# Last up-projection unit to first down products: where three operand casts and two weight casts stand in the queues

## Chip, cores and metric

One Trainium2 chip, one core. The metric is device time in microseconds (us), median over runs. The engines' names are those of the profile: PE (matrix multiplication), PEld (its weight loads), DVE (vector), ACT (scalar), POOL (GpSimd), SP (the queue that issues most DMA transfers). Each engine works through its own instructions strictly in the order in which the compiled program lists them, and an instruction that waits holds all behind it.

## What is computed

One layer for 1024 prompt frames and 32 sample frames (T = 1056 columns here): attention and a gated recurrence side by side, then a convolutional feed-forward block, then a gated per-layer input. The change lies in the feed-forward block:

```python
hf = _rms_norm(x, g_pre_ffn)
a, u = jnp.split(hf @ w_up, 2, axis=-1)          # 1024 -> 2 * 2816
ap = jnp.concatenate([prev, a], axis=1)
ac = b_conv
for j in range(CONV_W):                          # depthwise conv3
    ac = ac + ap[:, j:j + t] * w_conv[j]
ffn = (jax.nn.gelu(ac, approximate=True) * u) @ w_down   # 2816 -> 1024
x = x + _rms_norm(ffn, g_post_ffn)
```

All is float32. PE multiplies in a rounded format, so each operand is split in a rounded part (a cast on ACT) and the rest (a subtraction on DVE), and each product is three matmuls: rounded times rounded, rounded times rest, rest times rounded.

## The kernel before

**Up units.** The up-projection runs in 22 units u = 0..21 (NF = 22), each 128 columns of `a` and of `u`. A unit multiplies by a seven-product scheme (sums of quarter blocks stand in for the eighth product): `up_unit` goes through seven steps, each with a weight part `wt` of 4 x 128 x 128, two halves p of the tokens (264 columns each, on 128 partitions), in three PSUM tiles X, Y, Z. One step is 24 matmuls of 128x264. Behind its steps a unit leaves a tail, `ff_tail`: on DVE the scaling of u (L2264), the last sum out of PSUM (L2401) and its scaling into `ab` (L2405, L2408), copies of a few columns (L2254 to L2257); then the convolution, one tap on ACT (L2258) and two on DVE (L2262, L2266), the gelu on ACT (L2267), the product with u on DVE (L2271), a store. For all but the last unit this tail runs beside the next unit's matmuls.

**Down products.** The down-projection takes the same scheme over three groups of rows of `w_down`. The first group (pt = 0) has 3 blocks of 128 in each part. It runs in two phases: the products i = 0, 1, 2 for the column groups c = 0..3, then i = 3..6. So the down parts in order are: part 0, 1, 2 for c = 0; 3, 4, 5 for c = 1; 6, 7, 8 for c = 2; 9, 10, 11 for c = 3. One part is 18 matmuls. `d_unit` runs the products of one c: product 0 goes to PSUM tile X, product 1 to Y, and product 2 is added onto X. In between, `evacuate` copies X as it stands after product 0 to `S` on ACT (L2514), so that **product 2 of a c can't start before the `S` copy of that c has read X**. Y goes to `T`, and X after product 2 to `acc`, both also L2514 on ACT.

**Operands.** Product i needs two operand tiles `dop` (p = 0, 1), loaded by POOL's queue (`load_op`), cast on ACT (L2344) and completed on DVE (L2345) by `split_ops`. A weight part needs a raw tile `wd` (one tile holds two parts, two buffers, loaded by SP's queue, L2124), a cast on ACT (L2135) into a `wt` tile, and the rest on DVE (L2136): `d_prepare`. The `wt` tiles rotate over eight buffers, so that a cast may also have to wait for PE to finish with an old part. A third raw tile can be loaded only when both parts of the tile two before it have been cast and completed.

**What sets the order.** Instructions stand in a queue in the order in which the scheduler of the compiler puts them, from the order in which they are written; `behind(E)` keeps what is written under it behind the last instruction written so far for that engine. In the last unit (u = 21) the loads and casts of the first down products stand between the steps.

The functions around the change:

Of the kernel before, what the change touches and what calls it, by code (L numbers as in the profile page):

```python
# [59 lines left out]
def layer_kernel(  # L60
# [17 lines left out]
    def nm(s):  # L78
        n_names[0] += 1
        return f"{s}_{n_names[0]}"  # L80
# [5 lines left out]
    V, S, G, E = nc.vector, nc.scalar, nc.gpsimd, nc.tensor  # L86

    def behind(*engines):

        st = ExitStack()  # L90
        for e in engines:
            ins = next(i for i in reversed(nc.cur_bb.bb.instructions) if i.engine == e.engine)
            st.enter_context(tc.issue_after(ins))
        return st
# [1955 lines left out]
    def part_tile(i=0):  # L2050
        return wp.tile([P, 2, 4, P], F32R, tag="wb", name=nm("wt"), bufs=8)
# [62 lines left out]
    def d_raw():  # L2114

        k = len(raw_d)
        t = wp.tile([P, KT, P], F32, tag="wr", name=nm("wd"), bufs=2)
        raw_d.append(t)
        for a in range(2):
            pt, c, i = D_ORDER[2 * k + a]  # L2120
            j0, n = KP[pt]
            z_ = slice(j0, j0 + n)
            src = w_d[i][:, c, z_] if i in w_d else dv[:, i // 2 % 2 + i // 5, i // 5, c, z_]
            dma(t[:, 4 * a:4 * a + n], src)  # L2124

    def d_prepare(n):

        while len(ready_d) < min(n + 1, len(D_ORDER)):
            k = len(ready_d)
            while len(raw_d) < min(k // 2 + 2, len(D_ORDER) // 2):  # L2130
                d_raw()
            ng = KP[D_ORDER[k][0]][1]
            src = raw_d[k // 2][:, 4 * (k % 2):4 * (k % 2) + ng]
            t = part_tile()
            S.copy(t[:, 0, :ng], src)  # L2135
            V.tensor_tensor(t[:, 1, :ng], src, t[:, 0, :ng].bitcast(F32), op=ALU.subtract)  # L2136
            ready_d.append(t)
# [140 lines left out]
    def tail_rest(u):  # L2278
        for t in tail_of:
            next(t)  # L2280
        if u != 1:
            tail_of.clear()
# [58 lines left out]
    def split_op(pt, p, i):  # L2341
        n = KP[pt][1]
        hi, lo = (ops[p][i][:, a, :n] for a in range(2))
        S.copy(hi, lo.bitcast(F32))  # L2344
        V.tensor_tensor(lo, lo.bitcast(F32), hi.bitcast(F32), op=ALU.subtract)  # L2345

    def split_ops(pt, i, ps=(0, 1)):
        for p in ps:
            with behind(S, V):
                split_op(pt, p, i)  # L2350
# [3 lines left out]
    def up_unit(u):  # L2354
        X, Y, Z = (pf.tile([P, 2, 512], F32, tag="st", name=nm("st"), bufs=3) for _ in range(3))
        ab = fp.tile([P, 4 + T], F32, tag="ab", name=nm("ab"), bufs=2)
        G.memset(ab[:, 0:2], 0.0)
        us = us0 if u == 0 else Up[:, u % 2, :].bitcast(F32)
        us4 = us.rearrange("p (a h c) -> p a h c", a=2, h=2)
        w = {}  # L2360

        def mults(i, t, first, ps):
            n = 7 * u + i
            if i not in w:
                w[i] = ready_w[n]
            for p in ps:
                for k in range(4):
                    wh, wl = w[i][:, 0, k, :], w[i][:, 1, k, :]
                    xh, xl = ops[p][i][:, 0, k, :], ops[p][i][:, 1, k, :]
                    o = t[:, p, 0:H]  # L2370
                    E.matmul(o, wh, xh, start=first and k == 0, stop=False, skip_group_check=True)  # L2371
                    E.matmul(o, wh, xl, start=False, stop=False, skip_group_check=True)  # L2372
                    E.matmul(o, wl, xh, start=False, stop=k == 3, skip_group_check=True)  # L2373

        def v(t, ps):
            return t[:, ps[0]:ps[-1] + 1, 0:H]

        def after(i, ps):
            x, y, zz = v(X, ps), v(Y, ps), v(Z, ps)
            sl = slice(ps[0], ps[-1] + 1)  # L2380
            s1 = s10[:].unsqueeze(1) if u == 0 and ps == (0,) else s1c[:, sl]
            if i == 0:
                S.copy(s1, x)  # L2383
            elif i == 1:
                V.tensor_tensor(U2[:, sl], s1, y, op=ALU.subtract)
            elif i == 2:
                V.tensor_tensor(ab[:, 2:2 + T].rearrange("p (a h c) -> p a h c", a=2, h=2)[:, sl, 0, :],
                                x, rb4[:, sl, 0, :], op=ALU.mult)
            elif i == 3:
                V.tensor_tensor(nU3[:, sl], y, s1, op=ALU.subtract)  # L2390
            elif i == 4:
                V.tensor_tensor(us4[:, sl, 1, :], nU3[:, sl], zz, op=ALU.subtract)
            elif i == 5:
                V.tensor_tensor(us4[:, sl, 0, :], y, s1, op=ALU.subtract)
            elif i == 7:

                S.copy(t12[:, sl], zz)
            elif i == 8:
                V.tensor_tensor(nU3[:, sl], nU3[:, sl], t12[:, sl], op=ALU.add)
            else:  # L2400
                V.tensor_tensor(t12[:, sl], U2[:, sl], zz, op=ALU.add)  # L2401

        def done():

            V.tensor_tensor(ab[:, 2:2 + T].rearrange("p (a h c) -> p a h c", a=2, h=2)[:, :, 1, 0:232],  # L2405
                            t12[:, :, 0:232], rb4[:, :, 1, 0:232], op=ALU.mult)
            for p, o in ((0, 2 + 496), (1, 2 + 1026)):
                V.tensor_tensor(ab[:, o:o + 32], t12[:, p, 232:H], rb4[:, p, 1, 232:H], op=ALU.mult)  # L2408
            tail_of.append(ff_tail(u, ab, us))
            next(tail_of[0])  # L2410


        order = ((0, X, True, (0,)), (1, Y, True, (1,)), (2, X, False, (2,)), (3, Y, False, (3,)),
                 (4, Z, True, (4,)), (5, Y, False, (5,)), (6, Z, False, (6,)))
        first_ = order[:2] + ((2, X, False, ()),) + order[3:6] + ((6, Z, False, (2, 6)),)
        early = ((0, X, True, (0,)), (6, Z, True, (7,)), (2, X, False, ()), (1, Y, True, (1,)),
                 (3, Y, False, (3, 8)), (4, Z, False, (4, 6)), (5, Y, False, (2, 5)))
        for ps, steps in (((0,), first_), ((1,), early)) if u == 0 else (((0, 1), order),):
            for n, (i, t, first, then) in enumerate(steps):
                if u == NF - 1 and n == 0:  # L2420
                    d_raw()
                    d_raw()
                if u:
                    prepare(min(7 * u + n + AHEAD, 7 * NF - 1))
                    if u == NF - 1 and n:
                        d_prepare(n - 1)
                elif ps == (1,):
                    with behind(S, V):
                        prepare(n + AHEAD + 2)
                mults(i, t, first, ps)  # L2430
                if u == NF - 1:
                    if i < 3:
                        for p in range(2):
                            load_op(0, p, i, gdma)
                    if n in (3, 5, 6):
                        split_ops(0, {3: 0, 5: 1, 6: 2}[n])
                if ps == (1,) and n == 1:
                    with behind(E):
                        x1_t.append(pair_norm(1, 1.0 / D, late=True))
                if ps == (1,) and n == 4:  # L2440
                    with behind(E):
                        x1_t[0]()
                for a in then:
                    with behind(*((V,) if ps == (0,) and a == 2 else ())):
                        after(a, ps)
                if n == 1:
                    with behind(V):
                        tail_rest(u)
                if u == 1 and n == 3:
                    with behind(V):  # L2450
                        tail_rest(0)
                if u > 1 and n == 2 + u % 2:
                    if u % 2 == 0:
                        sums_of.append(act_sums(u // 2 - 1))
                    with behind(V):
                        next(sums_of[-1])
                if u == 0 and ps == (0,):
                    last_ops(n)
                if 2 <= u < 18 and n in (1, 4):
                    w_sum((u - 2) // 2, 2 * (u % 2) + n // 4)  # L2460
        done()

    Up = None
    for u in range(NF):
        if u == 1:
            Up = page(lq, 2, [P, 2, T], "Up")
        up_unit(u)
    tail_rest(NF)
    fctx.close()
    foctx.close()  # L2470
# [476 lines left out]
```

## Time and profile before

| what | value |
|---|---|
| time, median of 3 runs | 1944.42 us (1942.07, 1944.42, 1945.03) |
| the profiled execution's own time | 1947.46 us |
| its span, that is first to last instruction | 1945.8 us |
| mean granted PE clock | 0.996 |
| PE busy, of the span | 99% |
| DVE, ACT, POOL busy, of the span | 76%, 53%, 20% |
| last matmul of the last up unit starts at | 1602.00 us |
| matmuls of the down products | from 1602.1 to 1832.8 us |

The profiled execution is 3.04 us longer than the median of the runs, 1.66 us of it outside the span. Times of rows below count from the span's start. A row of the timeline gives start, duration, engine, line, output and inputs, shapes, and in brackets how long the engine had been idle before it and what released it. PE's rows overlap: a matmul of 128x264 lasts 0.28 us, and one starts about every 0.12 us.

### The profile page before, as it was taken

To read this page: it belongs to the slowest core of one execution; us is meant where nothing else is said; L and a number is where in the kernel's file an instruction comes from. 1 tells how busy PE (TensorE), PEld (TensorE's weight loads), DVE (VectorE), ACT (ScalarE), POOL (GpSimd) and SP (SyncE) were. 2 spreads that over 40 slices of the span, in tenths; PEclk is the share of its full clock that TensorE was granted. 3 is DMA by queue.
4 is the path that set the end of the run, shared out by engine and by line. 5 is a ranking of instruction groups with operands and counts; after the bars stand their busy time and mean duration, and the time that the engine had idled before them with its cause. 6 is when DMAs were issued, how large, how long until landed. Compare 5 with 4: busy or idle time off the path is not lost.

```text
span 1945.8 us, 38169 instructions
## 1 busy us (share of the span) xinstructions
PE 1921.6 (99%) x14523; PEld 1903.9 (98%) x14523; DVE 1472.6 (76%) x3201; ACT 1028.7 (53%) x2214; POOL 381.4 (20%) x530
## 2 busy tenths in 40 slices
PE   8999999999999999999999999999999999999999
PEld 7999999999999999999999999999999999999998
DVE  5777777788888888755796878777787786768872
ACT  6667778666666666553445763333333336534432
POOL 2111211000101010132321113444644330000000
PEclk9999999999999999999999999999999999999999
DMA  8544443445547364498979684566897356755343
GB/s 267 150 111 129 127 131 90 149 114 139 146 106 162 118 122 101 129 312 272 293 203 296 230 280 131 161 171 188 158 187 183 115 186 215 220 178 159 117 131 88
DMA packets 319599, 329.11 MB, mean 169 GB/s; under 512 B 17432, under 2 KB 277435, under 8 KB 319416
## 3 DMA queue, kind: packets, MB, share of 16 engines
q1 hardware_dynamic: 274152, 218.92, 36.4%
q0 software_dynamic: 45136, 107.70, 23.1%
q8 instruction: 114, 1.87, 0.4%
q14 instruction: 69, 0.57, 0.1%
q10 hardware_dynamic: 128, 0.06, 0.0%
HBM read 234.48 MB, written 132.47 MB: 189 GB/s over the span
## 4 chain that ended last, share of the span: by engine, by line
PE 85%; DVE 6%; DMA 3%; ACT 3%; issue 2%; POOL 0%; SPq 0%; ACTq 0%; DVEq 0%; POOLq 0%
PE st L2373 7%; PE st L2372 7%; PE st L2371 7%; PE mm L205 4%; PE mm L206 4%; PE mm L207 4%; PE st L2499 4%; PE st L2501 4%; PE st L2500 4%; PE st L1663 2%; PE st L1665 2%; PE st L1667 2%; PE st L205 2%; PE st L206 2%; PE st L207 2%
## 5 line engine op out<-in xcount | busy, mean ns | idle before, releaser
L2373 PE MATMUL st<-op,wt 128*128 128x264 f32 x1232 | 349.9, 284 | 0.0
L2371 PE MATMUL st<-op,wt 128*128 128x264 f32 x1232 | 348.7, 283 | 1.2 <-ACT Sp L2383 0.5
L2372 PE MATMUL st<-op,wt 128*128 128x264 f32 x1232 | 347.8, 282 | 0.0
L2371 PEld LDWEIGHTS st<-op,wt 128*128 128x128 f32 x1232 | 231.3, 188 | 2.5 <-ACT Sp L2383 0.9
L2372 PEld LDWEIGHTS st<-op,wt 128*128 128x128 f32 x1232 | 231.5, 188 | 0.0
L2373 PEld LDWEIGHTS st<-op,wt 128*128 128x128 f32 x1232 | 230.9, 187 | 0.0
L2499 PE MATMUL st<-dop,wt 128*128 128x264 f32 x616 | 175.2, 285 | 2.6 <-ACT S L2514 2.6
L2501 PE MATMUL st<-dop,wt 128*128 128x264 f32 x616 | 175.0, 284 | 0.0
L2500 PE MATMUL st<-dop,wt 128*128 128x264 f32 x616 | 174.7, 284 | 0.0
L2030 ACT CAST wt<-wu 128x512 fp32r<-128x512 f32 x126 | 76.0, 618 | 176.4 <-POOL wu L2039 71.5
L205 PE MATMUL mm<-La,wh 128*128 128x384 f32 (+1 forms) x480 | 158.3, 330 | 0.0
L206 PE MATMUL mm<-Lb,wh 128*128 128x384 f32 (+1 forms) x480 | 155.2, 324 | 0.2 <-DVE Lb L784 0.2
L207 PE MATMUL mm<-La,wl 128*128 128x384 f32 (+1 forms) x480 | 155.0, 323 | 0.1
L2031 DVE TENSOR_TENSOR wt<-wu,wt 128x512 fp32r<-128x512 f32 x126 | 86.4, 694 | 46.0 <-ACT wt L2030 46.0
L2499 PEld LDWEIGHTS st<-dop,wt 128*128 128x128 f32 x616 | 116.3, 189 | 3.1 <-ACT S L2514 3.0
L2500 PEld LDWEIGHTS st<-dop,wt 128*128 128x128 f32 x616 | 116.5, 189 | 0.0
L2501 PEld LDWEIGHTS st<-dop,wt 128*128 128x128 f32 x616 | 116.2, 189 | 0.0
L2135 ACT CAST wt<-wd 128x512 fp32r<-128x512 f32 (+1 forms) x84 | 48.9, 586 | 90.8 <-PE st L2501 70.7
L206 PEld LDWEIGHTS mm<-Lb,wh 128*128 128x128 f32 x480 | 90.5, 189 | 0.8 <-DVE Lb L784 0.5
L207 PEld LDWEIGHTS mm<-La,wl 128*128 128x128 f32 x480 | 90.3, 188 | 0.5 <-DVE wl L759 0.5
L1122 PE MATMUL G<-La,wt 128*128 128x288 f32 x288 | 90.4, 314 | 0.0
L205 PEld LDWEIGHTS mm<-La,wh 128*128 128x128 f32 x480 | 90.4, 188 | 0.0
(628 smaller groups left out, 6328.2 us busy)
## 6 DMA issues: line engine op xcount, KB each, us to landing
wu<-in_w_up_dram SPq DMA_DIRECT2D x42, 512.0 KB
wu<-in_w_in_dram SPq DMA_DIRECT2D x36, 512.0 KB
w_d<-in_w_down_dram POOLq DMA_DIRECT2D x24, 704.0 KB, 8.4
a_d<-Up SPq DMA_DIRECT2D x21, 528.0 KB
wr<-in_w_in_dram SPq DMA_DIRECT2D x21, 512.0 KB
s_d<-sm SPq DMA_DIRECT2D x40, 264.0 KB
dop<-s_d SPq DMA_DIRECT2D x16, 528.0 KB
wr<-in_w_out_dram SPq DMA_DIRECT2D x16, 512.0 KB
```

Source lines behind the costliest of these rows:

```text
L205: E.matmul(ps, wh, a, start=first and n == 0, stop=False)
L206: E.matmul(ps, wh, b, start=False, stop=False)
L207: E.matmul(ps, wl, a, start=False, stop=last and n == len(ks) - 1)
L1122: E.matmul(o, wh, x[0][k], start=first and k == 0, stop=False, skip_group_check=True)
L2030: S.copy(t[:, 0], src)
L2031: V.tensor_tensor(t[:, 1], src, t[:, 0].bitcast(F32), op=ALU.subtract)
L2371: E.matmul(o, wh, xh, start=first and k == 0, stop=False, skip_group_check=True)
L2372: E.matmul(o, wh, xl, start=False, stop=False, skip_group_check=True)
L2373: E.matmul(o, wl, xh, start=False, stop=k == 3, skip_group_check=True)
L2499: E.matmul(o, wh, xh_, start=first and k == 0, stop=False, skip_group_check=True)
L2500: E.matmul(o, wh, xl_, start=False, stop=False, skip_group_check=True)
L2501: E.matmul(o, wl, xh_, start=False, stop=k == ng - 1, skip_group_check=True)
```

## The change

The casts of the operand of product i = 2 (`split_ops(0, 2)`: two casts on ACT, two subtractions on DVE) are no longer written inside the last unit's seventh step, in front of that unit's last sums; they are written behind the whole unit. The casts of the down parts 6 and 7 (`d_prepare(6)`, `d_prepare(7)`), which were first written in `d_unit`, are written behind these and in front of `tail_rest(NF)`, which is what remains of the last unit's tail.

```diff
                     if n in (3, 5, 6):
-                        split_ops(0, {3: 0, 5: 1, 6: 2}[n])
+                        if n < 6:
+                            split_ops(0, {3: 0, 5: 1}[n])
...
     up_unit(u)
+    split_ops(0, 2)
+    for n in (6, 7):
+        with behind(V):
+            d_prepare(n)
     tail_rest(NF)
```

The number of instructions on each engine is the same before and after. Line numbers behind the change grow by 5 (L2499, L2514 become L2504, L2519). In the rows below, `dop_19765` and `dop_19767` are the operand of product 2 for the two halves; `wt_19875` is down part 5; `wt_19959` and `wt_19987` are the parts 6 and 7 before, `wt_19920` and `wt_19923` the same parts now, and both come from the raw tile `wd_19840`; `st_19933` (now `st_19942`) is X of c = 0, `st_20011` is X of c = 1.

ACT's queue, from the end of the last up unit on, before:

```order
L2135 CAST wt_19875<-wd_19773 128x384
L2344 CAST dop_19765<-dop_19765 128x792
L2344 CAST dop_19767<-dop_19767 128x792
L2514 COPY S_19932<-st_19933 128x528
L2258 ACTIVATE a_19910<-ab_19655,cvec 128x1058
L2135 CAST wt_19959<-wd_19840 128x384
L2267 ACTIVATE a_19910<-a_19910 128x1058
L2514 COPY S_19932<-st_20011 128x528
L2514 COPY T_19930<-st_19934 128x528
L2135 CAST wt_19987<-wd_19840 128x384
```

and now:

```order
L2135 CAST wt_19875<-wd_19773 128x384
L2135 CAST wt_19920<-wd_19840 128x384
L2135 CAST wt_19923<-wd_19840 128x384
L2258 ACTIVATE a_19906<-ab_19655,cvec 128x1058
L2344 CAST dop_19765<-dop_19765 128x792
L2344 CAST dop_19767<-dop_19767 128x792
L2519 COPY S_19941<-st_19942 128x528
L2267 ACTIVATE a_19906<-a_19906 128x1058
L2519 COPY S_19941<-st_20011 128x528
L2344 CAST dop_19963<-dop_19963 128x792
L2519 COPY T_19939<-st_19943 128x528
```

The two weight casts and the tail's first tap (L2258) now stand in front of the operand casts and of the first `S` copy; before, the operand casts and the copy stood in front of them.

DVE's queue at the same place, as the difference between the two kernels (L2264 to L2257, unchanged, are left out between the two pieces); first the piece that loses the operand's rests:

```order
 L2394 TENSOR_TENSOR Up_15042<-st_19653,Sp_14756 128x2x264
-L2345 TENSOR_TENSOR dop_19765<-dop_19765 128x792
-L2345 TENSOR_TENSOR dop_19767<-dop_19767 128x792
 L2264 TENSOR_TENSOR Up_15042<-Up_15042,rbT 128x1056
 L2401 TENSOR_TENSOR Sp_14756<-Sp_14756,st_19654 128x528
```

then the piece that takes them in:

```order
+L2262 SCALAR_TENSOR_TENSOR a_19906<-ab_19655,cvec,a_19906 128x1058
+L2345 TENSOR_TENSOR dop_19765<-dop_19765 128x792
+L2345 TENSOR_TENSOR dop_19767<-dop_19767 128x792
+L2136 TENSOR_TENSOR wt_19920<-wd_19840,wt_19920 128x384
+L2136 TENSOR_TENSOR wt_19923<-wd_19840,wt_19923 128x384
+L2266 SCALAR_TENSOR_TENSOR a_19906<-ab_19655,cvec,a_19906 128x1058
```

The four subtractions now stand between the two taps L2262 and L2266.

PE's queue around product 2 of c = 0, now (before, all 18 matmuls of the part stood in a row behind product 1; the rows here are the end of seven matmuls of part 3 and what follows):

```order
L2504 MATMUL st_20011<-dop_19690,wt_19812 128x264
L2504 MATMUL st_19942<-dop_19765,wt_19776 128x264
L2505 MATMUL st_20011<-dop_19690,wt_19812 128x264
L2505 MATMUL st_19942<-dop_19765,wt_19776 128x264
L2506 MATMUL st_19942<-dop_19765,wt_19776 128x264
```

Seven matmuls of part 3 (c = 1, product 0) have moved ahead of product 2 of c = 0.

## Prediction

> **What bounds the kernel now.** I read the page first, then PE's waits, its timeline from the last up unit on, the busy table by stretches, and last the timelines of ACT, DVE and SP at the same place.
>
> ```profile
> PE 1921.6 (99%) x14523; PEld 1903.9 (98%) x14523; DVE 1472.6 (76%) x3201; ACT 1028.7 (53%) x2214; POOL 381.4 (20%) x530
> PE 85%; DVE 6%; DMA 3%; ACT 3%; issue 2%; POOL 0%; SPq 0%; ACTq 0%; DVEq 0%; POOLq 0%
> PE st L2499 <- ACT S L2514: 2.6, 2, 1.9
> ```
>
> PE is busy for 99% of the span and carries 85% of the chain that ended last. So an edit counts only by the gaps it opens or closes on PE. The third row (waits: total, times, longest) says that in the whole stage of down products PE stands still twice, both times for an `S` copy. PE's timeline shows where:
>
> ```profile
> 1602.13 0.28 PE L2499 MATMUL st<-dop,wt 128*128 128x264 f32 x1
> 1610.70 0.28 PE L2501 MATMUL st<-dop,wt 128*128 128x264 f32 x1
> 1611.67 0.39 PE L2499 MATMUL st<-dop,wt 128*128 128x264 f32 x1 [0.69 <-ACT S L2514]
> 1620.36 0.28 PE L2501 MATMUL st<-dop,wt 128*128 128x264 f32 x1
> 1622.53 0.39 PE L2499 MATMUL st<-dop,wt 128*128 128x264 f32 x1 [1.90 <-ACT S L2514]
> ```
>
> From 1602.13 to 1610.70 four parts of 18 matmuls start, 71 steps in 8.57 us: 0.1207 us each, 2.17 a part. The first gap is 0.97 - 0.12 = 0.85 us (product 2 of c = 1), the second 2.17 - 0.12 = 2.05 us (product 2 of c = 2). The table by stretches (PE, PEld, DVE, ACT, POOL busy with counts, granted clock, DMA share, GB/s) shows a second price of the gaps:
>
> ```profile
> 909.98:913.40 3.42, 1.17 (x10) 1.20 (x11) 2.42 (x4) 1.85 (x3) 0.00 (x0) 1.00 0.36 105
> 913.40:916.81 3.41, 3.41 (x18) 3.41 (x17) 2.03 (x4) 0.00 (x0) 2.36 (x4) 0.51 0.78 231
> 1609.65:1613.06 3.41, 2.72 (x23) 2.51 (x22) 2.25 (x5) 3.09 (x6) 0.34 (x1) 1.00 0.02 6
> 1619.89:1623.30 3.41, 1.51 (x13) 1.30 (x12) 2.04 (x4) 3.41 (x8) 0.54 (x1) 1.00 0.44 165
> 1623.30:1626.71 3.41, 3.41 (x18) 3.41 (x18) 3.25 (x5) 2.67 (x6) 0.00 (x0) 0.52 0.46 135
> 1626.71:1630.13 3.42, 3.42 (x30) 3.42 (x29) 1.94 (x4) 3.02 (x7) 0.00 (x0) 0.98 0.63 191
> ```
>
> A stretch with 10 or 13 matmuls is followed by 3.4 us at half the clock, one with 23 is not. A half-clock stretch does 18 matmuls where a full one does 30 to 31: 12.5 x 0.1207 = 1.5 us. The stretches lie on a fixed grid, so whether a gap of 2 us falls into one or is shared by two should depend on the phase. The profiled execution is 3.04 us above the median of the runs, and it holds two such losses, 3.0 together; I take it that the median run has none to one of them and charge the one at 1623.30 to the before at half, 0.75 us.
>
> The Trainium skill (TensorE: Matmul & The Clock Gate, What's actually happening) says that the clock halves after at least one idle window of about 3.4 us; the trace disagrees, since 1.51 us of work in the 3.41 before did not prevent it. By that rule the old gap would cost no clock and the new one below would in most phases, and the sum would be about 0.5 us higher.
>
> **What ACT, DVE and SP do there.**
>
> ```profile
> 1596.93 1.61 ACT L2344 CAST dop<-dop 128x792 fp32r<-128x792 f32 x2
> 1605.45 0.60 ACT L2514 COPY S<-st 128x528 f32<-128x528 f32 x1 [6.92 <-DVE ab L2408]
> 1605.95 1.28 ACT L2258 ACTIVATE a<-ab,cvec 128x1058 f32<-128x1058 f32 x1
> 1607.31 0.52 ACT L2135 CAST wt<-wd 128x384 fp32r<-128x384 f32 x1
> 1609.97 1.09 ACT L2267 ACTIVATE a<-a 128x1058 f32<-128x1058 f32 x1 [2.14 <-DVE a L2266]
> 1611.02 0.60 ACT L2514 COPY S<-st 128x528 f32<-128x528 f32 x1
> 1619.39 0.52 ACT L2135 CAST wt<-wd 128x384 fp32r<-128x384 f32 x1 [3.28 <-DMA wd<-w_d]
> 1621.88 0.60 ACT L2514 COPY S<-st 128x528 f32<-128x528 f32 x1
> ...
> 1600.20 0.70 DVE L2394 TENSOR_TENSOR Up<-st,Sp 128x528 f32<-128x528 f32 x1
> 1600.82 1.87 DVE L2345 TENSOR_TENSOR dop<-dop 128x792 fp32r<-128x792 f32 x2
> 1602.60 1.25 DVE L2264 TENSOR_TENSOR Up<-Up,rbT 128x1056 f32<-128x1056 f32 x1
> 1603.77 0.70 DVE L2401 TENSOR_TENSOR Sp<-Sp,st 128x528 f32<-128x528 f32 x1
> 1605.46 0.16 DVE L2257 COPY ab<-cach 128x2 f32<-128x2 f32 x1
> 1607.26 1.32 DVE L2262 SCALAR_TENSOR_TENSOR a<-ab,cvec,a 128x1058 f32<-128x1058 f32 x1 [1.64 <-ACT a L2258]
> 1608.62 1.32 DVE L2266 SCALAR_TENSOR_TENSOR a<-ab,cvec,a 128x1058 f32<-128x1058 f32 x1
> 1614.04 1.03 DVE L2136 TENSOR_TENSOR wt<-wd,wt 128x384 fp32r<-128x384 f32 x2
> ...
> 1596.35 0.54 SPq L2124 DMA_DIRECT2D wd<-in_w_down_dram  x1
> 1597.61 0.45 SPq L2124 DMA_DIRECT2D wd<-w_d  x1
> 1600.31 1.00 SPq L2124 DMA_DIRECT2D wd<-in_w_down_dram  x2
> 1614.62 0.34 SPq L2124 DMA_DIRECT2D wd<-w_d  x1
> ```
>
> The second gap has a plain history: the parts 6 and 7 were completed on DVE only at 1614.04 to 1615.07, so SP could issue the raw tile of part 10 only at 1614.62; it landed at 1619.39, ACT sat 3.28 us in front of its cast, and the `S` copy of c = 2 behind it came at 1621.88.
>
> SP's own waits between its issues at 1600.31 and 1614.62 tell when the raw tile of the parts 6 and 7 landed, because the next load into the same buffer waits for both halves in turn:
>
> ```profile
> SPq L2124 <- DMA wd<-in_w_down_dram: 6.0, 1, 6.0
> SPq L2124 <- DVE nrm L2632: 5.3, 1, 5.3
> SPq L2124 <- DMA wd<-w_d: 1.9, 1, 1.9
> ```
>
> From 1601.31 (1600.31 + 1.00) the waits are 6.0, then 1.9, then 5.3, which makes 1614.5, the next issue. So part 6 landed at 1607.3 and part 7 at 1609.2, some 11 us after their issue. ACT's row at 1607.31 fits: that cast of part 6 starts 0.08 us after L2258 ends, where other rows start 0.1 before the end of the one ahead.
>
> **The change part by part.** No instruction is added; all effects are order.
>
> *DVE, the two operand rests leave the tail's front.* L2264 can follow L2394 at 1600.9 instead of 1602.60; but L2401 reads the last up product, whose last matmul starts at 1602.00, so it runs from about 1602.35 instead of 1603.77. `ab` is ready at 1604.2 instead of 1605.6: 1.4 us earlier, if ACT could use it.
>
> *ACT, the weight casts in front.* It can't. The casts of parts 6 and 7 now stand ahead of L2258, and the second waits for its data until 1609.2. Behind it are queued L2258, both operand casts and the `S` copy of c = 0, which PE needs. In row durations, each start 0.1 us before the end ahead: cast 1609.25, L2258 1609.67 to 1610.95, operand casts 1610.84 to 1612.45, `S` copy 1612.34 to 1612.94. PE resumes at 1613.0.
>
> *PE, first gap.* Parts 0 and 1 and seven matmuls of part 3 are ready without this: 43 x 0.1207 behind 1602.13 is 1607.32. The gap is 5.7 us, where before product 2 of c = 0 ran without one. 29 matmuls follow (18 of part 2, 11 of part 3) before product 2 of c = 1: 3.5 us, to 1616.6 at full clock. A gap of 5.7 us leaves at least one stretch of the grid emptier than the 13-matmul one, so I charge a half-clock stretch here: 1618.1.
>
> *DVE, four subtractions between the taps.* L2262 starts at 1610.98; 1.24 + 1.78 + 0.95 later L2266, to 1616.27; gelu to 1617.4; then the `S` copy of c = 1, which also needs part 3 from PE (1618.1 + 0.16 to its end): 1618.25 to 1618.85. Product 2 of c = 1 starts at 1618.85, before at 1611.67: **+7.2 us**; without a half clock the gelu would hold it to 1618.0, +6.35.
>
> *SP, part 10's raw tile.* It is issued when part 7 is complete, at 1615.05 instead of 1614.62, while PE stands 7 us earlier in its work than then. Its cast comes behind `T` of c = 1, at about 1624.4, when it has landed even at the 4.75 us that it took. The `S` copy of c = 2 then follows PE's product 0 and two casts at about 1626.6 to 1627.2, and PE asks for it at 1628.0: **the second gap goes, -2.05 us, and half of its clock loss, -0.75.** What covers it is 0.8 us of slack; if that fails, each us comes back.
>
> Sum: 7.2 - 2.05 - 0.75 = +4.4 us on the median, **1948.8 us** (+0.23%). In the profiled execution, with its clock loss in full, +3.65: 1951.1.
>
> Bounds: the landing moves the sum one to one. Earliest, the cast of part 6 must wait for PE to finish part 0 in its `wt` buffer, 18 x 0.1207 + 0.16 behind 1602.13, 1604.5. The same chain from there starts product 2 of c = 1 at 1613.7: +2.0 - 2.05 - 0.75 = -0.8 us. Latest, I take the landing 1.5 us later and one more half-clock stretch, +7.4. I stay with the row, since neither the issue of these loads nor what DMA moves beside them changes.
>
> **The rivals.**
>
> *The weights are there in time (not slower).* If the raw tile lands by 1604.5, the sum is the lower bound: 1943.6. Below a landing of about 1608.7 the loss is under 0.2%, which is about what a measurement of this kernel can tell from no change. For it: the load is only 192 KB. Against it: SP's waits and the late cast at 1607.31. The Trainium skill (DMA: Bandwidth & Descriptors, Anatomy of one DMA) gives about 2.0 us plus size by 436 GB/s, an estimate of 2.5 us here; no row here shows it: by SP's waits these took 11.0 and 11.6.
>
> *The clock stays low for longer (slower).* The gap may leave two stretches in a row too empty: 1.5 us more, 1950.3. For it: 5.7 us is more than one stretch of 3.4. Against: the gelu chain hides 0.7 us of the loss.
>
> *The last sums come late (slower).* They run on DVE behind L2271, which moves from 1611.09 to about 1617.4, and their stores must land before the `acc` copy of c = 2 may overwrite the tile. I put that copy at 1630, about when they land; a miss would pass through 2 us of slack in front of the `S` copy of c = 3. Price 0 to 2 us, 1950.8.
>
> *Nothing is held and both gaps go (faster).* The tail ends earlier and the copies come in time: 0.85 + 2.05 + 0.75, 1940.8. It needs the copy of c = 0 not to stand behind the casts, and the queue says that it does.
>
> **How the numbers follow.** Landing as in the trace, sum between +3 and +6: 0.60, of which 0.45 is slower by over 0.2% (3.9 us) and 0.15 within it. Weights clearly earlier: 0.20, within. Longer low clock or late sums: 0.13, slower. Faster case: 0.07, some of it within. Together slower 0.57, same 0.37, faster 0.06. The range runs from 1942.8, the in-time case with the old clock loss charged in full, to 1952.5, the latest landing with 0.7 us of late sums.
>
> **What would show it.** PE waiting some 5.7 us for ACT's `S` copy from 1607.3; ACT waiting for the raw tile in front of L2135 until about 1609.2; L2266 near 1615; half clock behind the gap; no wait of PE at product 2 of c = 2. If ACT's weight casts run at 1604 to 1606, the prediction is wrong at the landing; if PE's gap is there but the time is unchanged, at what I charge for the old one.

## The result and the profile after

The changed kernel takes 1950.24 us in the median of 7 runs (1948.18 to 1955.35), the kernel before 1944.4 (1942.07 to 1945.78, 7 runs): ratio 1.0033, 95% interval 1.0022 to 1.0043. A second series of the changed kernel, 8 runs, gave 1.0028 (1.0016 to 1.0040). So it is slower by 5 to 6 us in the medians, 0.3%, and both intervals lie clear of 1; 4.4 us were forecast. The profiled execution shown here is one of the long ones: 1952.98 us, span 1951.3; 1951.1 were forecast for it.

PE's waits (in total, times, longest) and the rows of its timeline at and behind the wait:

```profile
PE st L2504 <- ACT S L2519: 7.6, 2, 7.0
1613.68 0.59 PE L2504 MATMUL st<-dop,wt 128*128 128x264 f32 x1 [6.95 <-ACT S L2519]
1614.51 0.42 PE L2506 MATMUL st<-dop,wt 128*128 128x264 f32 x1
1618.69 0.42 PE L2506 MATMUL st<-dop,wt 128*128 128x264 f32 x1
1619.11 0.29 PE L2505 MATMUL st<-dop,wt 128*128 128x264 f32 x1
1620.56 0.39 PE L2504 MATMUL st<-dop,wt 128*128 128x264 f32 x1 [0.69 <-ACT S L2519]
```

There are again two gaps, and the wait is again for an `S` copy; but the first is now product 2 of c = 0, and it is 7 us long. Product 2 of c = 2, which waited 1.90 us before, has no wait. ACT's timeline shows why:

```profile
1607.82 0.51 ACT L2135 CAST wt<-wd 128x384 fp32r<-128x384 f32 x1 [11.54 <-DMA wd<-in_w_down_dram]
1609.96 0.51 ACT L2135 CAST wt<-wd 128x384 fp32r<-128x384 f32 x1 [1.63 <-DMA wd<-w_d]
1610.38 1.26 ACT L2258 ACTIVATE a<-ab,cvec 128x1058 f32<-128x1058 f32 x1
1611.55 1.59 ACT L2344 CAST dop<-dop 128x792 fp32r<-128x792 f32 x2
1613.05 0.59 ACT L2519 COPY S<-st 128x528 f32<-128x528 f32 x1
1616.99 1.09 ACT L2267 ACTIVATE a<-a 128x1058 f32<-128x1058 f32 x1 [3.36 <-DVE a L2266]
1619.91 0.60 ACT L2519 COPY S<-st 128x528 f32<-128x528 f32 x1 [1.83 <-PE st L2506]
1627.85 0.61 ACT L2519 COPY S<-st 128x528 f32<-128x528 f32 x1
```

ACT is idle for 11.54 and 1.63 us in front of the casts of the parts 6 and 7. Then it works without a pause through the tap, the operand casts and the `S` copy. DVE's rows show that the tap had its data since 1603.5, and that L2262 sat 8.14 us idle behind ACT:

```profile
1603.37 0.16 DVE L2257 COPY ab<-cach 128x2 f32<-128x2 f32 x1
1611.68 1.32 DVE L2262 SCALAR_TENSOR_TENSOR a<-ab,cvec,a 128x1058 f32<-128x1058 f32 x1 [8.14 <-ACT a L2258]
1615.64 1.32 DVE L2266 SCALAR_TENSOR_TENSOR a<-ab,cvec,a 128x1058 f32<-128x1058 f32 x1
```

SP had issued the two halves of that raw tile long before:

```profile
1595.92 0.38 SPq L2124 DMA_DIRECT2D wd<-in_w_down_dram  x1
1596.99 0.43 SPq L2124 DMA_DIRECT2D wd<-w_d  x1
```

From issue to cast that is 11.9 us for part 6 and 13.0 for part 7. The table by stretches (PE, PEld, DVE, ACT, POOL busy, granted clock, DMA share, GB/s) shows the clock:

```profile
1608.00:1609.00 1.00, 0.00 (x0) 0.00 (x0) 0.00 (x0) 0.33 (x1) 0.00 (x0) 0.91 0.39 106
1609.00:1613.00 4.00, 0.00 (x0) 0.00 (x0) 1.32 (x2) 3.04 (x4) 0.00 (x0) 0.50 0.03 8
1614.00:1618.00 4.00, 4.00 (x19) 4.00 (x19) 2.96 (x4) 1.01 (x1) 0.00 (x0) 0.50 0.24 76
1619.00:1620.00 1.00, 0.87 (x7) 0.67 (x6) 1.00 (x4) 0.09 (x1) 0.26 (x1) 0.97 0.00 0
```

The granted clocks of 0.91 and 0.97 at the two ends place the half clock from about 1608.8 to 1619.1, three stretches of the grid. Behind the gap some 24 matmuls start every 0.22 us instead of every 0.12: 2.4 us.

To compare kernels I take the down stage alone, from the start of its first matmul to the start of its last, since the start of the stage scatters between profiled executions by 4.6 us (1598.75 to 1603.38), although little ahead of it differs. A part of this scatter goes with half clock: six of the eleven profiles have a half-clock stretch somewhere between 877 and 917, as the one at 913.40 before, and reach the stage at 1600.69 to 1603.38; the other five, without it, at 1598.75 to 1600.83. "Rest" is the length without PE's waits for ACT.

| kernel | first, last down matmul | length | PE waits | rest |
|---|---|---|---|---|
| before | 1602.13, 1832.82 | 230.69 | 2.6 | 228.1 |
| changed | 1601.38, 1838.06 | 236.68 | 7.6 | 229.0 |
| changed, second series | 1602.09, 1837.17 | 235.08 | 6.1 | 229.0 |
| operand casts alone | 1600.83, 1829.42 | 228.59 | 1.6 | 227.0 |
| weight casts alone | 1600.69, 1834.45 | 233.76 | 4.9 | 228.8 |
| changed, early raw tile | 1599.46, 1827.60 | 228.14 | 1.1 | 227.0 |
| weight casts alone, early raw tile | 1603.38, 1830.86 | 227.48 | 0.8 | 226.7 |
| changed, early raw tile, weight rests first | 1599.68, 1827.17 | 227.49 | 0.8 | 226.7 |
| changed, POOL's loads late | 1598.75, 1830.85 | 232.10 | 4.8 | 227.3 |
| changed, spare matmuls | 1599.66, 1833.09 | 233.43 | 2.4 | 231.0 |
| changed, spare matmuls, second series | 1603.34, 1836.71 | 233.37 | 2.3 | 231.1 |

### The profile page after: what moved, and what is told of

Read it like the earlier page. It is cut to its first block, busy times and chain, and to the rows that moved or that the text cites. A ratio compares the mean times of both kernels' runs of the same rounds, so it can differ in the third digit from the quotient of the medians.

```text
span 1951.3 us, 38166 instructions
## 1 busy us (share of the span) xinstructions
PE 1923.4 (99%) x14523; PEld 1904.4 (98%) x14523; DVE 1473.6 (76%) x3201; ACT 1028.2 (53%) x2214; POOL 382.2 (20%) x530
## 4 chain that ended last, share of the span: by engine, by line
PE 85%; DVE 6%; DMA 3%; ACT 3%; issue 2%; SPq 0%; POOL 0%; ACTq 0%; DVEq 0%; POOLq 0%
PE st L2373 7%; PE st L2372 7%; PE st L2371 7%; PE mm L205 4%; PE mm L206 4%; PE mm L207 4%; PE st L2504 4%; PE st L2506 4%; PE st L2505 4%; PE st L1663 2%; PE st L1665 2%; PE st L1667 2%; PE st L205 2%; PE st L206 2%; PE st L207 2%
## 5 line engine op out<-in xcount | busy, mean ns | idle before, releaser
L2504 PE MATMUL st<-dop,wt 128*128 128x264 f32 x616 | 175.5, 285 | 7.6 <-ACT S L2519 7.6
L2504 PEld LDWEIGHTS st<-dop,wt 128*128 128x128 f32 x616 | 116.7, 190 | 8.2 <-ACT S L2519 8.1
```

The lines of the kernel that those rows point to most:

```text
L2504: E.matmul(o, wh, xh_, start=first and k == 0, stop=False, skip_group_check=True)
```

## The experiments

**Which of the two moves costs?** First the operand casts alone are moved; `d_prepare` of 6 and 7 stays in `d_unit`:

```diff
     up_unit(u)
     split_ops(0, 2)
-    for n in (6, 7):
-        with behind(V):
-            d_prepare(n)
     tail_rest(NF)
```

> Half of the change: the casts of the operand of product 2 are written behind the last unit, the weight casts of parts 6 and 7 stay where they were before. Theory (ACT waits for the raw tile of parts 6 and 7 in front of the first S copy): no weight cast stands ahead of that copy now, so PE waits at most 0.5 us at product 2 of c = 0, the second gap of about 2 us at c = 2 stays, and the time is that of before plus 0.4 us, 1944.8 (+-1.5). Rival (the price is the operand casts standing behind the tail's first tap): most of the loss is here, a gap of 3 us or more at product 2 of c = 0 and 1948 to 1950.

Measured: 1943.03 us (11 runs), ratio 0.9997 (0.9988 to 1.0006). PE's waits in the down stage:

```profile
PE st L2501 <- ACT S L2516: 1.6, 2, 0.9
```

No large gap and no change of the time. The gap at c = 2, expected to stay at some 2 us, came out at 0.86. Then the weight casts alone; the operand casts are back in the seventh step:

```diff
-                        if n < 6:
-                            split_ops(0, {3: 0, 5: 1}[n])
+                        split_ops(0, {3: 0, 5: 1, 6: 2}[n])
...
     up_unit(u)
-    split_ops(0, 2)
     for n in (6, 7):
```

> The other half: the operand casts stay in the unit, the weight casts of parts 6 and 7 stand in front of the tail and of the S copy of c = 0. Theory: the second weight cast waits for its data until 1609 to 1610, the S copy behind it ends near 1610.3, PE waits 3.8 us at product 2 of c = 0, product 2 of c = 1 starts 4.4 to 5.2 us later than before, the second gap goes: 1.5 to 2.5 us over before, 1946 to 1947. Rival (the operand casts are the price): no gap at c = 0, the second gap gone, 2 to 3 us under before, 1941.6.

Measured: 1948.04 us, ratio 1.0024 (1.0015 to 1.0033), a little more than expected. From the stage's start, product 2 of c = 1 comes 6.7 us later than before, where 4.4 to 5.2 were expected. ACT's casts and the first gap of PE:

```profile
1608.36 0.51 ACT L2135 CAST wt<-wd 128x384 fp32r<-128x384 f32 x1 [2.61 <-DMA wd<-w_d]
1608.78 0.59 ACT L2517 COPY S<-st 128x528 f32<-128x528 f32 x1
1609.42 0.59 PE L2502 MATMUL st<-dop,wt 128*128 128x264 f32 x1 [4.23 <-ACT S L2517]
```

So the loss sits with the weight casts. Here the `S` copy follows the late cast at once, 0.42 us behind its start; in the changed kernel it follows 3.1 us behind (1609.96 to 1613.05), since the tap and the operand casts are queued between. The clock is halved here too, from about 1607.5 to 1614.4.

**Order or late data?** The changed kernel with its whole order, but the raw tile of the parts 6 and 7 is loaded earlier, into a buffer that is free by then. SP issues its halves at 1578.38 and 1578.85, some 21 us ahead of the first down matmul, where the changed kernel issued them 5.5 and 4.4 us ahead of it; so the load is some 16 us earlier, not the planned 12:

```diff
-        t = wp.tile([P, KT, P], F32, tag="wr", name=nm("wd"), bufs=2)
+        pool, tag = (fp, "wx") if k == 3 else (wp, "wr")
+        t = pool.tile([P, KT, P], F32, tag=tag, name=nm("wd"), bufs=2)
...
+                        if n == 3:
+                            d_raw()
```

> The changed kernel with its queues on PE, ACT and DVE as they are, but the raw tile of parts 6 and 7 is loaded some 12 us earlier, into a buffer that the up units no longer need. Theory: the two weight casts wait only for PE to finish part 0 (1604.5), the S copy of c = 0 ends near 1608.6, gaps of 1.3 us at c = 0 and 1.5 at c = 1, none at c = 2, no half clock at most runs: 1943.6, that is 0.8 us under before and 5 to 7 under the changed kernel. Rival (it is the order of the casts, not their data): a gap of 5 us or more at c = 0, 1949 to 1950.

Measured: 1942.27 us (11 runs), ratio 0.9991 (0.9982 to 1.0000). Its ACT and PE:

```profile
1596.80 0.52 ACT L2136 CAST wt<-wd 128x384 fp32r<-128x384 f32 x1 [2.44 <-PE st L2374]
1599.71 0.52 ACT L2136 CAST wt<-wd 128x384 fp32r<-128x384 f32 x1 [2.39 <-PE st L2374]
1604.29 0.59 ACT L2522 COPY S<-st 128x528 f32<-128x528 f32 x1
1609.86 0.39 PE L2507 MATMUL st<-dop,wt 128*128 128x264 f32 x1 [1.12 <-ACT S L2522]
```

The same instructions stand in the same order ahead of the `S` copy, and the copy of c = 0 comes at 1604.29 instead of 1613.05. What it took away is the wait for the raw tile, and the loss went with it. The same tile under the weight casts alone:

> The weight casts in front of the tail, the operand casts in the unit, and the raw tile of parts 6 and 7 loaded early. Theory: the weight casts wait only for PE's part 0, the S copy of c = 0 ends at 1606 and PE has no gap there; DVE's tail is held until 1605 by the first weight's rest, so the gap at product 2 of c = 1 grows to 1.8 us; no gap at c = 2: 1.8 us under before, 1942.6. Rival (order alone): as the kernel with the weight casts alone, 1946 to 1947, if that one is slow.

Measured: 1943.59 us, ratio 0.9998 (0.9989 to 1.0007), with one gap:

```profile
1613.07 0.39 PE L2505 MATMUL st<-dop,wt 128*128 128x264 f32 x1 [0.83 <-ACT S L2520]
```

Here too the loss is gone; the time is 1 us above the expected one.

**Why does the tile take 12 us?** Around it, from 1591.67 to 1601.85, POOL's queue issues eight operand loads of 396 KB for the second phase. In this kernel one small POOL write into `ab`, which changes no value, stands ahead of them and holds them until the tap L2262 is done:

```diff
     tail_rest(NF)
+    G.memset(last_ab[0][:, 0:2], 0.0)
...
-            load_op(q, p, i, gdma if (pt, ph) == (0, 0) else dma)
+            with behind(*((G,) if (pt, ph) == (0, 0) else ())):
+                load_op(q, p, i, gdma if (pt, ph) == (0, 0) else dma)
```

> The changed kernel with POOL's eight operand loads of the second phase held until behind the tap L2262 (by one small POOL write that leaves the values as they are). Theory (SP's load of the raw tile lands 11 us after its issue because POOL's loads of 128x792 tiles are moved beside it): parts 6 and 7 land near 1600 to 1602, their casts run then, the first PE gap is 0 to 1.5 us, and the time is 1943 to 1945 unless the later operand loads open a gap of their own. Rival (these loads do not matter, other traffic of SP's queue or the queue itself does): the casts still end at 1608 to 1610.5, the first gap is 6 to 7 us, 1949 to 1951.

Measured: the issues of the two halves, the casts, PE's two largest gaps, and the late cast ahead of the second:

```profile
1592.80 0.38 SPq L2124 DMA_DIRECT2D wd<-in_w_down_dram  x1
1593.85 0.38 SPq L2124 DMA_DIRECT2D wd<-w_d  x1
1596.09 0.52 ACT L2135 CAST wt<-wd 128x384 fp32r<-128x384 f32 x1 [2.44 <-PE st L2375]
1599.00 0.52 ACT L2135 CAST wt<-wd 128x384 fp32r<-128x384 f32 x1 [2.39 <-PE st L2375]
1609.15 0.39 PE L2507 MATMUL st<-dop,wt 128*128 128x264 f32 x1 [1.12 <-ACT S L2522]
1619.73 0.51 ACT L2135 CAST wt<-wd 128x384 fp32r<-128x384 f32 x1 [3.98 <-DMA wd<-w_d]
1620.79 0.39 PE L2507 MATMUL st<-dop,wt 128*128 128x264 f32 x1 [2.66 <-ACT S L2522]
```

The casts now wait for PE, not for data: part 6 is there at most 3.3 us after its issue, part 7 at most 5.2, instead of 11.9 and 13.0. The DMA share in the same table by stretches, of the changed kernel and then of this one:

```profile
1596.00:1600.00 4.00, 4.00 (x35) 4.00 (x35) 4.00 (x7) 0.28 (x1) 2.27 (x3) 1.00 1.01 360
1600.00:1604.00 4.00, 4.00 (x35) 4.00 (x34) 3.46 (x9) 0.00 (x0) 1.52 (x2) 1.00 1.06 397
```

```profile
1592.00:1596.00 4.00, 4.00 (x36) 4.00 (x35) 4.00 (x7) 0.77 (x2) 0.00 (x0) 1.00 0.74 253
1596.00:1600.00 4.00, 4.00 (x36) 4.00 (x35) 3.62 (x6) 1.03 (x2) 0.00 (x0) 1.00 0.42 128
1600.00:1604.00 4.00, 4.00 (x34) 3.89 (x33) 2.60 (x8) 3.09 (x4) 0.09 (x1) 1.00 0.00 1
```

The first pair of rows is the changed kernel, whose tile is issued at 1595.92; with POOL's loads beside it the DMA share is 1.01 to 1.06. The other three rows are this kernel, whose tile is issued at 1592.80; while it is under way the share is 0.74, and then it falls. So POOL's loads fill the DMA engines, and SP's small load goes through with them. The Trainium skill (DMA: Bandwidth & Descriptors, Issuing engines are not separate DMA queues) says that transfers issued from different engines run on the same 16 DMA engines and interleave; this pair of traces agrees. The median time is 1948.08 us (12 runs), ratio 1.0021 (1.0011 to 1.0030), outside 1943 to 1945. The profile shows a new gap of 2.66 us at a later raw tile, issued at 1613.26 beside three of the held operand loads; its cast waited 3.98 us for the data until 1619.73. So the wait has moved to another tile; that the held loads are what slowed this one is read from the timing alone. This profiled execution took only 1945.66 us, the second shortest of the 12, and what made the median run 2.4 us longer isn't shown.

**What does the clock cost?** 36 spare matmuls, whose results nothing reads, stand in PE's queue ahead of product 2 of c = 0. Behind them the scheduler also put product 1 of c = 1 ahead of its product 2:

```diff
+            if (pt, ph, c, n) == (0, 0, 0, 2):
+                spare = tr_bank()
+                for _ in range(36):
+                    with behind(E):
+                        E.matmul(spare[:, 0:H], ready_d[3][:, 0, 0, :], ops[0][0][:, 0, 0, :],
+                                 start=True, stop=True, skip_group_check=True)
```

> The changed kernel with 36 spare matmuls of 128x264 (into an otherwise unused PSUM tile, nothing reads them) in PE's queue right ahead of product 2 of c = 0, so that PE is active in most of the gap. Behind it c = 1's product 1 also runs ahead of its product 2. Theory (the gap costs its 7 us of waiting and, on top, some 2.4 us of work at half clock behind it): the spare work lasts 36 x 0.12 = 4.3 us inside the gap, the wait for the S copy of c = 0 shrinks to about 2.5 to 3 us without moving its end, at most one half-clock stretch is left, and the second small gap goes: 1946.5 to 1948.5, some 2 us under the changed kernel. Rival (the half clock costs nothing, since the gelu chain would hold PE anyway): only the small gap of 0.7 us goes, 1949.5. Second rival (the spare work delays PE): over 1951.

```profile
1604.01 4.48 PE L2569 MATMUL tr<-dop,wt 128*128 128x264 f32 x36
1610.72 0.39 PE L2504 MATMUL st<-dop,wt 128*128 128x264 f32 x1 [2.23 <-ACT S L2519]
...
1608.00:1611.00 3.00, 0.77 (x7) 0.48 (x5) 2.29 (x3) 2.67 (x4) 0.00 (x0) 1.00 0.00 0
1611.00:1616.00 5.00, 4.82 (x38) 4.61 (x38) 3.85 (x5) 1.98 (x4) 0.00 (x0) 1.00 0.27 79
```

In the profile it does what was meant: full clock throughout the stage, and the rest of the stage, without the spare work of 36 x 0.1207, is 226.7 us against 229.0. So half clock costs some 2.3 us in the profiled execution, near the 2.4 of the 24 matmuls. But the median, 1949.18 us (11 runs, ratio 1.0027, 1.0019 to 1.0036), misses the expected 1946.5 to 1948.5. Both were run once more on one chip:

> The changed kernel once more, beside the kernel with the spare matmuls and on the same chip, to size the clock's part in the median run. The profiled run of the changed kernel had three half-clock stretches behind the gap and stood 2.7 us above its median. Theory: the waits are in every run (some 7.6 us in the down products against 2.6 before, +5.0), the half-clock stretches behind the gap number one to three by the phase of the grid; median 1949.5 to 1950.5, and a run with granted clock 0.999 or more stands near 1948. Rival (three stretches always): all runs at 0.997 or less, 1950.5 to 1953.

> The changed kernel with 36 spare matmuls ahead of product 2 of c = 0, again, on the same chip as the changed kernel. If the median run of the changed kernel pays for half-clock stretches, this one is 1 to 3 us under it (no half clock behind the gap, and 0.9 us less waiting); if the clock costs nothing in the median run, it is 0 to 0.5 us under it. Its granted clock should be 0.999 or 1.0 in nearly all runs.

Measured: 1950.4 us for the changed kernel (8 runs, granted clock 0.996 to 0.999), 1951.74 with the spare matmuls (6 runs, 0.998 to 0.999); ratios 1.0028 (1.0016 to 1.0040) and 1.0032 (1.0020 to 1.0044). The intervals overlap; the kernel with the spare matmuls came out 1.3 us longer, so neither the gain of 1 to 3 us nor that of 0 to 0.5 is seen. The second profile repeats the first: full clock, a stage of 233.37 us. So in the profiles the spare matmuls shorten the stage by 1.7 to 3.3 us, and in the medians they don't.

The profiles were unequal draws: those of the changed kernel stood 2.7 and 1.5 us above their medians, the first one with the spare matmuls was the shortest of its 11 runs. The granted clock that is on record for every run says more. Of the 15 runs of the changed kernel, the three at 0.999 took 1946.16 to 1949.36 us, the three at 0.996 1951.15 to 1955.35: runs with more half clock are longer. But the ten runs with spare matmuls at 0.999 took 1948.57 to 1952.12. That points to a cost of its own that no trace here explains, so the experiment isn't a clean removal of the half clock; what the half clock behind the gap costs in the median run stays open.

The second profile of the changed kernel is useful for another reason: its stage starts at 1602.09, where the forecast had taken it, 1602.13.

```profile
1609.08 0.51 ACT L2135 CAST wt<-wd 128x384 fp32r<-128x384 f32 x1 [2.64 <-DMA wd<-w_d]
1612.80 0.59 PE L2504 MATMUL st<-dop,wt 128*128 128x264 f32 x1 [5.36 <-ACT S L2519]
1619.67 0.39 PE L2504 MATMUL st<-dop,wt 128*128 128x264 f32 x1 [0.69 <-ACT S L2519]
...
1613.00:1618.00 5.00, 5.00 (x23) 5.00 (x24) 3.85 (x6) 1.09 (x1) 0.00 (x0) 0.50 0.29 79
```

**A version from these.** The changed kernel with the early raw tile, and the rests of these weights written ahead of the operand's:

```diff
     up_unit(u)
-    split_ops(0, 2)
     for n in (6, 7):
-        with behind(V):
-            d_prepare(n)
+        d_prepare(n)
+    split_ops(0, 2)
     tail_rest(NF)
```

> The changed kernel with the raw tile of parts 6 and 7 loaded some 12 us earlier into its own buffer, and the rests of these weights written ahead of the operand's rests. Theory (the loss is the late raw tile alone, and order costs nothing once it is there): no PE gap over 1.2 us in the down products, no half-clock stretch there, 1941.5 to 1943, under both the kernel before and the changed one. Rival (the order on DVE matters by itself: the weight rests in front hold the taps and so the S copies): a gap of 1 to 3 us at the first or second product 2, 1944.5 to 1947.

Measured: 1942.55 us (11 runs), ratio 0.9988 (0.9980 to 0.9997). One gap is left in the down products:

```profile
1609.36 0.39 PE L2506 MATMUL st<-dop,wt 128*128 128x264 f32 x1 [0.82 <-ACT S L2521]
```

It is faster than the kernel before by 0.6 to 3.9 us (the ends of the interval), and can't be told from the changed kernel with the early tile alone (0.9991).

## Why the prediction was right, and where its sizes were off

- **The hold on ACT: right, and shown.** The time is inside the range and near the forecast, 1.4 us above it; for the profiled execution 1951.1 were forecast, 1952.98 and 1951.89 measured. The order of the rows on ACT, the waiting cast and the copy behind it came as written; the early tile, with the same order, takes the loss away.
- **The landing: right to 0.7 us.** Forecast for the cast of part 7 1609.25; 1609.96 in the first profile, 1609.08 in the second. The rival that had the weights there in time quoted an estimate of 2.5 us for this load. The Trainium skill (DMA: Bandwidth & Descriptors, Anatomy of one DMA) gives the fit behind it for transfers on the GpSimd path; this load is SP's, and its halves took 11.9 and 13.0 us to their casts.
- **The first gap: 5.7 forecast, 5.36 and 6.95 measured.** In the first profile the stage began 0.75 us earlier and the data came 0.7 later, so the gap grew at both ends. The step had taken one execution's stage start against the same execution's landing; the two are not tied (from the first down matmul to the cast of part 7 it is 8.58 us in the first profile, 6.99 in the second), and the difference between them is the gap.
- **The clock: mis-sized.** One half-clock stretch, 1.5 us, was charged behind the gap. It was three stretches of the grid, two of them at least partly behind the restart, and about 24 matmuls at 0.22 us: 2.4 us. The second profile, where the other terms fit, isolates this: with the gap's end 0.2 us earlier than forecast, product 2 of c = 1 came 0.8 us later (1619.67 against 1618.85). The rival "the clock stays low for longer" was thus what the profiled executions did; how often in others is the open point above.
- **Product 2 of c = 1: +7.2 forecast.** From the stage's start, 9.54 us before (1611.67 - 1602.13), 19.18 and 17.58 after: +9.6 and +8.0. In the first, the gap's 1.25 and the clock's 0.9 make 2.15 of the 2.4 too little; in the second, the clock's 0.9 less 0.3 for a shorter gap makes 0.6 of the 0.8. For the profiled execution +3.65 had been forecast; the stage grew by 6.0 and 4.4, so this one term carries the whole error.
- **The second gap goes: right.** The `S` copy of c = 2 ran at 1627.85 and PE did not wait. The raw tile of part 10 was issued at 1615.79 (forecast 1615.05), and its cast at 1625.77 had no wait for data, while PE stood later in its work, as forecast.
- **The old clock loss:** the rest of the stage before, 228.1, lies 0.8 to 1.4 us above those of kernels without half clock in the stage (226.7 to 227.3), so the before's profiled execution paid about that, not 1.5. Its excess of 3.04 us over the median lies wholly in the span, since the other runs too are some 1.7 us longer than their spans.
- **The floor was wrong.** The lower bound had the cast of part 6 wait for PE to finish part 0, at 1604.5. With the data there (early tile, late POOL loads) PE released it during the last up unit, at 1596 to 1600. That the bound on the sum, -0.8 us, lies near what the early tile gave (0.9991, that is -1.7 us, interval -3.5 to 0.0) is luck, since the wait that it was worked out from didn't occur.
- **Late sums: no cost.** No wait of PE in the down stage came from them; only the two `S` copies appear.
- **In the whole:** waits +5.0 (7.6 against 2.6) and rest +0.9 make the stage's +6.0 us of the first profile; +3.5 and +0.9 the +4.4 of the second. The change is slower by 5.8 and 5.2 us in the medians, where +4.4 was forecast.

## What to carry to other kernels

A prefetch step on an engine that also empties PSUM is only free if its data have landed. Read when the load lands, from the waits of the queue that reuses its buffer, and not how small it is; then count what stands behind the waiting instruction. If the early place is wanted, move the load first: the same order with the tile loaded some 16 us sooner lost nothing. Before thinning another queue's traffic to speed up a load, look where that traffic goes instead: here a new gap stood 11.6 us behind the first one (1609.15 and 1620.79).

## What the runs showed of the hardware that I had not expected

- A gap of PE of 5.4 to 7 us is followed by more than the next grid stretch at half clock. The stretch in which PE restarts is itself partly empty, and the one behind it is half too: some 5.4 us of work at half clock behind each gap (1613.68 to 1619.1, and 1612.80 to 1618.2). The Trainium skill (TensorE: Matmul & The Clock Gate, What's actually happening) gives a free-running window of 3413 ns, and the three stretches of together 10.2 us agree; the same table has the clock come back after at least one busy window, and the third stretch, from 1615.65 on, is the first that PE works through. What its condition of an idle window doesn't cover is the first halving: the stretch ahead of 1608.8 held 1.33 us of work (12 matmuls).
- 36 matmuls that nothing reads, in the 6.7 us between the last useful matmul and the restart, kept the clock at 1.00, although the 2.23 us behind them were idle. The phase helped: reckoned in steps of 3.413 us (303 of them lie between the two beginnings of half clock in the second profile, 913.14 and 1947.38) from the half clock at the end of the span, a border of the grid falls into this idle time at about 1609.6, and the stretches on its two sides hold 2.35 and 2.25 us of work. In the second profile the emptier one holds 1.99. Whether the clock holds where all the idle time falls into one stretch, no run shows; in the kernel before, a stretch with 1.51 us of work was followed by half clock.
- A load of 192 KB takes at most 3.3 us from issue to use with POOL's operand loads held (share 0.74), and 11.9 beside loads that fill the DMA engines (share 1.01 to 1.06). These are the first halves of the raw tile; the second ones took at most 5.2 and 13.0.
- Profiled executions of kernels that differ little ahead of the down stage reach it at 1598.75 to 1603.38, in part by a half-clock stretch that some have and others have not. A scatter of this size hides any effect of 1 us unless many runs are compared, or the stage alone.
